# Relative-bias rows made in the first convolution layer and sent out from SBUF in sixteen pieces

## The chip, the cores and the metric

One Trainium2 chip, one core. The engines are TensorE (PE, with its weight loads PEld), VectorE (DVE), ScalarE (ACT) and GpSimd (POOL); SyncE (SP) issues nearly all DMA transfers, and 16 DMA engines move them. Each engine, and SP's queue, takes its instructions in order. The metric is the device time of one execution of the whole program in microseconds; the median of several runs counts.

## The reference

Two transformer blocks follow each other on 256 tokens of width 1024, batch 1, all in f32. The first block has two layers; each is a mixer and a convolutional feed-forward:

```
h = h + hgrn2_mixer(rms_norm(h))        # layer 0: a gated linear recurrence
h = h + conv_ffn(rms_norm(h))           # layer 0: (silu(conv(gate)) * conv(up)) @ w_down, conv of width 3
h = h + dsa_mixer(rms_norm(h))          # layer 1: attention on the 64 best keys of each query
h = h + conv_ffn(rms_norm(h))           # layer 1
```

The attention mixer scores all keys with 8 small index heads, keeps the top 64 keys of each query (`L // 4`), and does softmax attention with 16 heads over them. A bias that depends on the distance and the head is added to the logits:

```
rel = q_pos[None, :, None] - sel
bias = rel_bias.astype(jnp.float32)[t5_causal_bucket(rel)]     # rel_bias is (32 buckets, 16 heads)
logits = jnp.where(valid, logits + bias, NEG_BIG)
```

The second block (half-step SwiGLU layers, a gMLP mixer, a latent-attention mixer) is not touched.

## The kernel before

**Products.** Each f32 weight is split in two parts, `whi` and `wlo`, and each product is made of three matmuls (`whi` with both parts of x, `wlo` with one). A *unit* is one 1 MB tile of weights: `fetch` (line 207) issues its DMA on SP into one of three `wst` buffers, and `unit` (line 228) splits it: ACT copies `wst` to `whi` (line 249), DVE subtracts to get `wlo` (line 251). There are four `whi` and four `wlo` buffers. So the transfer of unit n is issued when DVE has split unit n-3, and ACT can split unit n when PE has finished unit n-4. A unit of a projection is 48 matmuls on PE (lines 263 to 265).

**The first convolution layer.** `conv_ffn` (line 663) loops over 11 pairs of gate and up units (22 units of `in_ffn_w_up`); after each unit DVE scales the sums (`cvx`, line 690) and DVE and ACT do the convolution (`cvg`, `cvu`, lines 671 to 673), the silu and the product, and split the result for the down projection (`in_ffn_w_down`, lines 565 to 567).

**The bias.** `rel_bias` (line 1044) is called after that layer. It loads a 0/1 table (`onehot`) and the 32 x 16 bias table (`rtab`), multiplies them on PE (line 1055) into 384 values for each head, copies them to SBUF (`rrow`, line 1057), and one DMA (line 1059) writes them to the DRAM tensor `bias_rows` of 16 heads x 128 query rows x 384: each head's row, which lies on one SBUF partition, is written 128 times over, 3 MB in all. The attention reads the bias back from there with a row step of 383 instead of 384, which shifts each query's row by one; these are 12 loads named `dx` (line 1166).

**The attention mixer.** `dsa` (line 1062) takes its units in this order: `dside` (keys and values), two units of index queries `dqi`, a half unit of values, and four units of queries (called q0 to q3 here; their results are `dq`, line 1152). The index scores are products on PE (line 1109), which ACT passes through a relu (`drl`, line 1112), and DVE sums over the index heads (`dsc`, lines 1116 and 1118) before it picks the 64 best (lines 1125 and 1126).

A scheduler sets the order of instructions on each engine when the program is built; `behind` (line 192) asks it not to place instructions ahead of PE's last one.

Of the kernel before, what the change touches and what calls it, by code (L numbers as in the profile page):

```python
# [7 lines left out]
F32 = mybir.dt.float32  # L8
# [7 lines left out]
P = 128  # L16
D = 1024
T = 256
KD = 8
# [3 lines left out]
NEG = -1e30  # L23
# [12 lines left out]

N_G, N_E, N_M, N_Z = 30, 4, 4, 2
N_SQ, N_WX, N_W, N_SM = 4, 3, 3, 3
ONCE = ("hrr", "hrh", "hrg", "dwt", "fgain", "f2", "mq1", "mq2", "mq3", "mq4", "mss", "dz")
N_TOP = 64  # L40
LEVELS = 5
CUTS = 4
# [76 lines left out]
C_ONEHOT = C_TRIL + P  # L119
# [28 lines left out]
class Net:  # L148
# [27 lines left out]
    def small(s, name, n):  # L176
        bufs = 1 if name in ONCE else N_SM
        return s.tp.tile([P, 16], F32, name=name, tag=name, bufs=bufs)[:, :n]
# [13 lines left out]
    def behind(s):  # L192

        pe = mybir.EngineType.PE
        return s.tc.issue_after(next(i for i in reversed(s.nc.cur_bb.bb.instructions) if i.engine == pe))

    def warm(s, n):

        if n:
            with s.behind():  # L200
                ps = s.prod()
                x = s.ident.bitcast(BF16)
                for _ in range(n):
                    s.nc.tensor.matmul(ps[:, :T], x[:, :P], x, start=True, stop=True)
# [180 lines left out]
    def pre(s, gain):  # L385
        p = Net.Pre()
        p.gain, p.ss, p.halves = gain, s.small("pss", 8), False
        p.marks, p.turns = [], []
        p.x = Split(s, "x", KD)
        return p  # L390
# [272 lines left out]
    def conv_ffn(s, p, l, out):  # L663
        nc, a = s.nc, s.a
        w = a["ffn_w_up"][l]
        hid = Split(s, "f", KF)
        s.begin(p)

        def conv(y, x, c):
            taps = [s.vec("conv_w%d%d" % (i, l), c, 1) for i in range(3)]  # L670
            nc.scalar.activation(y, x, AF.Identity, scale=taps[2], bias=s.vec("conv_b%d" % l, c, 1))
            nc.vector.scalar_tensor_tensor(y[:, 1:], x[:, :T - 1], taps[1], y[:, 1:], op0=OP.mult, op1=OP.add)
            nc.vector.scalar_tensor_tensor(y[:, 2:], x[:, :T - 2], taps[0], y[:, 2:], op0=OP.mult, op1=OP.add)

        h2 = lambda x: x.rearrange("p (j t) -> p j t", j=2)
        for i in range(KF // 2):
            if l == 0 and i in (3, 6):

                if i == 3:
                    turns = s.conv_vectors(1)  # L680
                else:
                    with s.behind():
                        for turn in turns:
                            turn()
            ys = [s.e("cvg"), s.m("cvu")]
            for y, first in zip(ys, (0, KF)):
                c = first + 2 * i
                ps = s.feat2(s.unit([(w, c * P, T)], 0, KD), p.x)
                x = s.z("cvx")
                nc.vector.tensor_tensor(h2(x), h2(ps), s.rb2(p), op=OP.mult)  # L690
                for j in range(2):
                    half = slice(j * T, (j + 1) * T)
                    conv(y[:, half], x[:, half], c + j)
                if not first:
                    nc.scalar.activation(y, y, AF.Silu)
            g, u = ys
            nc.vector.tensor_tensor(u, u, g, op=OP.mult)
            s.split(hid.hi.pair(i), hid.lo.pair(i), u)
        s.down(a["ffn_w_down"][l], hid, KF, out)
# [344 lines left out]
    def rel_bias(s):  # L1044


        nc, a = s.nc, s.a
        onehot = s.e("onehot")[:, :384]
        tab = s.tmp("rtab", P)
        nc.sync.dma_start(onehot, a["consts"][:, C_ONEHOT:])  # L1050
        nc.gpsimd.memset(tab, 0.0)
        nc.gpsimd.memset(tab[32:64], NEG)
        nc.sync.dma_start(tab[:32, :16], a["rel_bias"])
        ps = s.mix()
        nc.tensor.matmul(ps[:, :384], tab, onehot, start=True, stop=True)
        row = s.m("rrow")[:, :384]
        nc.vector.tensor_copy(row, ps[:, :384])
        scr = s.dp.tile([16, P, 384], F32, name="bias_rows")
        nc.sync.dma_start(scr, row[:16][:, None, :].to_broadcast([16, P, 384]))
        s.bias_rows = scr  # L1060

    def dsa(s, p, out_):
        nc, a = s.nc, s.a
# [606 lines left out]
def run_net(tc, a, out, stop=99, debug=None):  # L1670
    with ExitStack() as ctx:
        s = Net(tc, ctx, a)
        nc = tc.nc

        def dump(name):
            if debug and name in debug:
                nc.sync.dma_start(debug[name].rearrange("(t p) d -> p t d", p=P), s.h)
            return stop <= int(name[1:])

        w = a["hgrn_w_in"][0]  # L1680
        p = s.start([(w, D), (w, D + T), (w, D + 2 * T)])
        dump("h0")
        nxt = s.hgrn(p, s.first)
        if dump("h1"):
            return
        p = s.pre_end(nxt)
        nxt = s.pre(s.vec("attn_norm", KD))
        s.conv_ffn(p, 0, s.residual(nxt))
        s.rel_bias()
        if dump("h2"):  # L1690
            return
        p = s.pre_end(nxt)
        nxt = s.pre(s.vec("ffn_norm", KD))
        s.dsa(p, s.residual(nxt))
        if dump("h3"):
            return
        p = s.pre_end(nxt)
        out1, end1 = s.block1_end(s.vec("final_norm"), a["final_norm"], s.vec("pre_g", 0))
        s.conv_ffn(p, 1, out1)
        if dump("h4"):  # L1700
            return
        p = end1()
        dump("h5")
        wg, wu, wd = (a["ffn_w_%s_2" % n] for n in ("gate", "up", "down"))

        def ffn(p, l, j, pres, beside=None, **kw):
            s.swiglu(p, wg[l, j], wu[l, j], wd[l, j], s.post(a["ffn_post_g_2"][l, j], pres, True, **kw), beside)

        pre = lambda l, j: s.pre(s.vec("pre_g", (2 * l + j) * KD))
        mixg = lambda n, l: s.vec(n, l * KD)  # L1710
        nxt = s.pre(mixg("mix_pre", 0))
        kn = []
        ffn(p, 0, 0, [nxt])
        if dump("h6"):
            return
        p, nxt = nxt, pre(0, 1)
        s.gmlp(p, s.post(a["mix_post_g_2"][0], [nxt]))
        if dump("h7"):
            return
        p, nxt, kv = nxt, pre(1, 0), s.pre(s.vec("kv_norm"))  # L1720
        ffn(p, 0, 1, [nxt, kv])
        s.rope_tables()
        if dump("h8"):
            return
        ckv = []
        p, nxt = nxt, s.pre(mixg("mix_pre", 1))
        ffn(p, 1, 0, [nxt], lambda: ckv.extend(s.shared_kv(kv)), fill=lambda: kn.append(s.k_heads(ckv)))
        if dump("h9"):
            return
        p, nxt = nxt, pre(1, 1)  # L1730
        s.mla(p, ckv, kn[0], s.post(a["mix_post_g_2"][1], [nxt], late=L_MLA))
        if dump("h10"):
            return
        dst = out.rearrange("o (t p) d -> p (o t) d", p=P)

        def done(n, t):
            cols = slice(n * T, (n + 1) * T)
            nc.sync.dma_start(dst[:, t, cols], s.h[:, t, cols])


        ffn(nxt, 1, 1, [], done=done)
# [34 lines left out]
```

## Time and profile before

| | |
|---|---|
| median of 3 runs | 1652.7 us (1647.62 to 1656.69) |
| the profiled execution: time | 1660.22 us |
| the profiled execution: span, first to last instruction | 1658.4 us |
| PE busy in the span | 1622.1 us (98%) |
| DVE busy | 1150.2 us (69%) |
| ACT busy | 913.1 us (55%) |
| mean DMA rate | 179 GB/s |

The profiled execution stands 7.5 us above the median of the runs. Busy shares are means over the whole span, over stages with different limits. "Granted clock" is TensorE's clock as a share of its upper level (2.4 GHz); 0.50 is the lower level, 1.2 GHz.

### The profile page before, as it was taken

The numbers are of one execution on the slowest core, as the hardware profiler recorded it, in microseconds if no ns is written. First come the engines' busy times: TensorE is split into PE (matmuls) and PEld (weight loads), VectorE is DVE, ScalarE is ACT, GpSimd is POOL, SyncE is SP. The second block draws the span as 40 slices with busy tenths as digits, with TensorE's granted clock in tenths as the row PEclk, the third lists the DMA queues.
The fourth block names the chain that finished last, engine by engine and source line by source line (L and its number), as shares of the span: only waits on it lengthen the run. The fifth ranks groups of instructions, "written<-read, shape, count | busy, mean of one in ns | idle before, by whom it ended". The sixth has DMA issues, their size and how long they took to land.

```text
span 1658.4 us, 34159 instructions
## 1 busy us (share of the span) xinstructions
PE 1622.1 (98%) x14500; PEld 1608.4 (97%) x14502; DVE 1150.2 (69%) x1900; ACT 913.1 (55%) x1443; POOL 6.7 (0%) x28
## 2 busy tenths in 40 slices
PE   8989999996999999999999999999999999999998
PEld 8979999995999999999999999999999999999998
DVE  6997899545769975766668757664676647576643
ACT  7876665443666555544466446444664448574442
POOL 0000000000000000000000000000000000000000
PEclk9999999997999999999999999999999999999999
DMA  8733655677546556556756556556475665446551
GB/s 266 220 97 114 200 178 188 191 141 177 157 149 208 173 181 216 182 186 217 231 161 211 168 175 197 186 169 206 130 233 189 193 201 151 132 153 212 189 190 58
DMA packets 303821, 297.58 MB, mean 179 GB/s; under 512 B 14295, under 2 KB 300214, under 8 KB 303670
## 3 DMA queue, kind: packets, MB, share of 16 engines
q1 hardware_dynamic: 303622, 295.40, 57.4%
q8 instruction: 114, 1.87, 0.5%
q14 instruction: 37, 0.30, 0.1%
q10 hardware_dynamic: 48, 0.01, 0.0%
HBM read 291.19 MB, written 4.19 MB: 178 GB/s over the span
## 4 chain that ended last, share of the span: by engine, by line
PE 88%; DVE 4%; DMA 3%; ACT 3%; issue 1%; SPq 0%; DVEq 0%; ACTq 0%
PE acc L263 16%; PE acc L265 16%; PE acc L264 16%; PE acc L565 8%; PE acc L567 7%; PE acc L566 7%; PE acc L289 2%; PE acc L290 2%; PE acc L291 2%; DMA bias_rows<-rrow 2%; PE acc L576 2%; PE acc L578 2%; PE acc L577 2%; DVE wlo L251 1%; ACT whi L249 1%
## 5 line engine op out<-in xcount | busy, mean ns | idle before, releaser
L249 ACT ACTIVATE whi<-wst 128x2048 fp32r<-128x2048 f32 (+4 forms) x404 | 523.8, 1330 | 517.5 <-issue 228.6
L251 DVE TENSOR_TENSOR wlo<-wst,whi 128x2048 fp32r<-128x2048 f32 (+4 forms) x404 | 621.0, 1561 | 251.6 <-ACT whi L249 249.6
L264 PE MATMUL acc<-xl,whi 128*128 128x256 f32 x2416 | 675.2, 280 | 1.1 <-DVE xl L308 1.1
L263 PE MATMUL acc<-xh,whi 128*128 128x256 f32 x2416 | 675.3, 281 | 0.8 <-ACT xh L306 0.4
L265 PE MATMUL acc<-xh,wlo 128*128 128x256 f32 x2416 | 674.7, 280 | 0.5 <-DVE wlo L251 0.5
L264 PEld LDWEIGHTS acc<-xl,whi 128*128 128x128 f32 x2416 | 458.1, 190 | 1.7 <-DVE xl L308 1.5
L265 PEld LDWEIGHTS acc<-xh,wlo 128*128 128x128 f32 x2416 | 455.0, 189 | 0.9 <-DVE wlo L251 0.7
L263 PEld LDWEIGHTS acc<-xh,whi 128*128 128x128 f32 x2416 | 454.3, 188 | 1.6 <-ACT xh L306 0.7
L567 PE MATMUL acc<-wlo,fh 128*128 128x256 f32 x880 | 245.3, 279 | 0.0
L565 PE MATMUL acc<-whi,fh 128*128 128x256 f32 x880 | 244.7, 279 | 0.0
L566 PE MATMUL acc<-whi,fl 128*128 128x256 f32 x880 | 244.5, 278 | 0.0
L567 PEld LDWEIGHTS acc<-wlo,fh 128*128 128x128 f32 x880 | 165.2, 188 | 0.0
L565 PEld LDWEIGHTS acc<-whi,fh 128*128 128x128 f32 x880 | 165.0, 188 | 0.0
L566 PEld LDWEIGHTS acc<-whi,fl 128*128 128x128 f32 x880 | 164.9, 187 | 0.0
L289 PE MATMUL acc<-whi,xh 128*128 128x256 f32 x384 | 108.9, 284 | 0.0
L291 PE MATMUL acc<-wlo,xh 128*128 128x256 f32 x384 | 106.8, 278 | 0.0
L290 PE MATMUL acc<-whi,xl 128*128 128x256 f32 x384 | 106.8, 278 | 0.0
L289 PEld LDWEIGHTS acc<-whi,xh 128*128 128x128 f32 x384 | 72.1, 188 | 0.2
L290 PEld LDWEIGHTS acc<-whi,xl 128*128 128x128 f32 x384 | 72.1, 188 | 0.0
L291 PEld LDWEIGHTS acc<-wlo,xh 128*128 128x128 f32 x384 | 72.1, 188 | 0.0
L658 DVE TENSOR_TENSOR ffu<-acc,rb 128x512 f32<-128x512 f32 x41 | 28.3, 691 | 48.5 <-PE acc L265 48.3
L308 DVE SCALAR_TENSOR_TENSOR xl<-mx,vectors,xh 128x128 fp32r<-128x128 f32 (+1 forms) x124 | 39.1, 376 | 23.1 <-ACT xh L306 23.0
(422 smaller groups left out, 2097.3 us busy)
## 6 DMA issues: line engine op xcount, KB each, us to landing
wst<-in_ffn_w_up_dram SPq DMA_DIRECT2D x88, 1024.0 KB, 5.2
wst<-in_ffn_w_down_dram SPq DMA_DIRECT2D x48, 1024.0 KB, 5.9
wst<-in_ffn_w_gate_dram SPq DMA_DIRECT2D x44, 1024.0 KB, 5.4
wst<-in_ffn_w_down_dram SPq DMA_DIRECT2D x24, 768.0 KB, 4.8
wst<-in_gmlp_w_in_dram SPq DMA_DIRECT2D x16, 1024.0 KB, 5.4
wst<-in_hgrn_w_in_dram SPq DMA_DIRECT2D x13, 1024.0 KB, 5.5
wst<-in_gmlp_w_out_dram SPq DMA_DIRECT2D x8, 1024.0 KB
wst<-in_dsa_w_in_dram SPq DMA_DIRECT2D x6, 1024.0 KB
```

Of the source, the lines that this page charges most:

```text
L249: s.nc.scalar.activation(hi[:, c], w[:, c], AF.Copy)
L251: s.nc.vector.tensor_tensor(lo[:, c], w[:, c], hi[:, c].bitcast(F32), op=OP.subtract)
L263: mm(ps, wh[:, k, cols], xh, start=k == 0, stop=False)
L264: mm(ps, wh[:, k, cols], xl, start=False, stop=False)
L265: mm(ps, wl[:, k, cols], xh, start=False, stop=k == nk - 1)
L289: mm(ps, xh[:, ts], wk, start=k == 0, stop=False)
L290: mm(ps, xl[:, ts], wk, start=False, stop=False)
L291: mm(ps, xh[:, ts], lk, start=False, stop=k == nk - 1)
L308: b = s.nc.vector.scalar_tensor_tensor(lo, src, g, hi.bitcast(F32), op0=OP.mult, op1=OP.subtract)
L565: mm(ps[t], xh, wh[:, k], start=k0 + k == 0 and not both, stop=False)
L566: mm(ps[t], xl, wh[:, k], start=False, stop=False)
L567: mm(ps[t], xh, wl[:, k], start=False, stop=k0 + k == kn - 1 and (t == 1 or not both))
```

## The change

`rel_bias` now makes no instruction by itself: it returns a list of 18 steps, which `conv_ffn` of layer 0 takes one by one. The first loads the two tables (in the pair of units i = 1, behind the fetch of its gate unit), the second is the product on PE and the copy to `rrow` (i = 1, up unit), and the other sixteen each write 8 query rows of all 16 heads to `bias_rows`, 192 KB, one behind the fetch of each unit from i = 3 to i = 10. `after_fetch` asks the scheduler not to place a step ahead of SP's last DMA. `rrow` has a buffer of its own, of which only 16 partitions are copied; the room comes from three small tiles (`ss2`, `gmv`, `grs`) that now have one buffer instead of three. The bytes that are written are the same.

```diff
-ONCE = ("hrr", "hrh", "hrg", "dwt", "fgain", "f2", "mq1", "mq2", "mq3", "mq4", "mss", "dz")
+ONCE = ("hrr", "hrh", "hrg", "dwt", "fgain", "f2", "mq1", "mq2", "mq3", "mq4", "mss", "dz", "ss2", "gmv", "grs")
...
+    def after_fetch(s):
+
+        sp = mybir.EngineType.SP
+        return s.tc.issue_after(next(i for i in reversed(s.nc.cur_bb.bb.instructions) if i.engine == sp))
...
+        bias = s.rel_bias() if l == 0 else []
...
-                ps = s.feat2(s.unit([(w, c * P, T)], 0, KD), p.x)
+                u = s.unit([(w, c * P, T)], 0, KD)
+                if bias and (i > 2 or i and len(bias) > 16):
+                    with s.after_fetch():
+                        bias.pop(0)()
+                ps = s.feat2(u, p.x)
...
-        ps = s.mix()
-        nc.tensor.matmul(ps[:, :384], tab, onehot, start=True, stop=True)
-        row = s.m("rrow")[:, :384]
-        nc.vector.tensor_copy(row, ps[:, :384])
+        row = s.tp.tile([P, 384], F32, name="rrow", tag="rrow", bufs=1)
         scr = s.dp.tile([16, P, 384], F32, name="bias_rows")
-        nc.sync.dma_start(scr, row[:16][:, None, :].to_broadcast([16, P, 384]))
         s.bias_rows = scr
...
+        def product():
+            onehot, tab = parts
+            with s.behind():
+                ps = s.mix()
+                nc.tensor.matmul(ps[:, :384], tab, onehot, start=True, stop=True)
+            nc.vector.tensor_copy(row[:16], ps[:16, :384])
+
+        def spread(q):
+            nc.sync.dma_start(scr[:, q:q + 8], row[:16][:, None, :].to_broadcast([16, 8, 384]))
+
+        return [load, product] + [lambda q=q: spread(q) for q in range(0, P, 8)]
...
         s.conv_ffn(p, 0, s.residual(nxt))
-        s.rel_bias()
```

SP's queue around the attention mixer before: the write of `bias_rows` stands ahead of the weights of q2 (the row behind it), the four `dx` loads of the first block of queries and the weights of q3.

```order
L216 DMA wst<-in_dsa_w_in_dram 128x8x128
L216 DMA wst<-in_dsa_w_in_dram 128x8x256 x2
L1059 DMA bias_rows<-rrow 2048x1x384
L216 DMA wst<-in_dsa_w_in_dram 128x8x256
L1166 DMA dx<-bias_rows 128x4x128 x4
L216 DMA wst<-in_dsa_w_in_dram 128x8x256
L216 DMA wst<-in_dsa_w_out_dram 128x8x256 x3
```

The same place in the changed program:

```order
L221 DMA wst<-in_dsa_w_in_dram 128x8x128
L221 DMA wst<-in_dsa_w_in_dram 128x8x256 x3
L1187 DMA dx<-bias_rows 128x4x128 x4
L221 DMA wst<-in_dsa_w_in_dram 128x8x256
L221 DMA wst<-in_dsa_w_out_dram 128x8x256 x3
```

The write has left the place; q0, q1 and q2 follow each other, and the rest keeps its order.

SP's queue in the up projection of the first convolution layer, changed program, from the first of the 22 units on; before, the 22 `wst` loads stand here with `rtab` behind the third and nothing else between them:

```order
L221 DMA wst<-in_ffn_w_up_dram 128x8x256 x3
L1068 DMA rtab<-in_rel_bias_dram 32x16
L465 DMA vst<-in_ffn_conv_w_dram 44x128
L465 DMA vst<-in_ffn_conv_b_dram 44x128
L221 DMA wst<-in_ffn_w_up_dram 128x8x256 x4
L1065 DMA onehot<-in_consts_dram 128x384
L221 DMA wst<-in_ffn_w_up_dram 128x8x256 x2
L1079 DMA bias_rows<-rrow 16x8x384 x3
L221 DMA wst<-in_ffn_w_up_dram 128x8x256
L1079 DMA bias_rows<-rrow 16x8x384
```

Three pieces stand behind the ninth unit's load, and from there each of the 13 other loads has one piece behind it. The two `vst` loads (convolution taps of layer 1) stood further ahead before.

DVE in the changed program, in the same stretch; the row on `rrow` is new here, and before it stood at the start of the attention mixer:

```order
L678 SCALAR_TENSOR_TENSOR cvu<-cvx,vectors,cvu 128x255 x2
L1076 COPY rrow<-mx 16x384
L256 TENSOR_TENSOR wlo<-wst,whi 128x2048
L700 TENSOR_TENSOR cvx<-acc,rb 128x512
L679 SCALAR_TENSOR_TENSOR cvu<-cvx,vectors,cvu 128x254 x2
```

One copy of 16 partitions is put between a convolution step and the split of the seventh unit. Further on in this layer the scheduler also places two `cvx` rows behind each other in most pairs, where they stood apart before.

## Rows read from the trace of the kernel before

**Rows 1.** The page: the chain that ended last, shares by engine and line.
```profile
PE 88%; DVE 4%; DMA 3%; ACT 3%; issue 1%; SPq 0%; DVEq 0%; ACTq 0%
PE acc L263 16%; PE acc L265 16%; PE acc L264 16%; PE acc L565 8%; PE acc L567 7%; PE acc L566 7%; PE acc L289 2%; PE acc L290 2%; PE acc L291 2%; DMA bias_rows<-rrow 2%; PE acc L576 2%; PE acc L578 2%; PE acc L577 2%; DVE wlo L251 1%; ACT whi L249 1%
```

**Rows 2.** The chain from 340 to 400 us: start, duration, what.
```profile
350.84 32.55 DMA bias_rows<-rrow
...
385.54 7.77 DMA wst<-in_dsa_w_in_dram
```

**Rows 3.** SP's timeline from 340 to 400 us: start, duration, line, transfer.
```profile
351.61 9.49 SPq L216 DMA_DIRECT2D wst<-in_dsa_w_in_dram  x1
383.41 2.02 SPq L1166 DMA_DIRECT2D dx<-bias_rows  x4
385.54 1.04 SPq L216 DMA_DIRECT2D wst<-in_dsa_w_in_dram  x1
```

**Rows 4.** ACT's timeline, same stretch; in brackets the idle time before and its releaser.
```profile
366.11 0.18 ACT L1088 ACTIVATE dwt<-mx 128x16 f32<-128x16 f32 x1
386.81 1.91 ACT L249 ACTIVATE whi<-wst 128x2048 fp32r<-128x2048 f32 x1 [20.51 <-DMA wst<-in_dsa_w_in_dram]
```

**Rows 5.** PE's timeline, same stretch.
```profile
368.17 1.05 PE L1109 MATMUL pr<-dki,dqi 128*128 128x128 f32 x8
...
372.60 0.28 PE L263 MATMUL acc<-xh,whi 128*128 128x256 f32 x1
389.04 2.07 PE L1109 MATMUL pr<-dki,dqi 128*128 128x128 f32 x8 [16.17 <-ACT drl L1112]
390.77 0.56 PE L264 MATMUL acc<-xl,whi 128*128 128x256 f32 x1
...
394.12 0.28 PE L264 MATMUL acc<-xl,whi 128*128 128x256 f32 x1
...
395.65 1.99 PE L1109 MATMUL pr<-dki,dqi 128*128 128x256 f32 x8 [0.30 <-ACT drl L1112]
```

**Rows 6.** Stretches: length, busy time of each engine, granted clock, DMA share, GB/s.
```profile
376.00:380.00 4.00, 0.00 (x0) 0.00 (x0) 0.00 (x0) 0.00 (x0) 0.00 (x0) 0.63 0.90 103
...
390.00:392.00 2.00, 2.00 (x12) 2.00 (x11) 1.86 (x4) 0.00 (x0) 0.00 (x0) 0.50 1.09 348
```

**Rows 7.** DVE's timeline from 355 to 450 us.
```profile
361.57 2.29 DVE L251 TENSOR_TENSOR wlo<-wst,whi 128x2048 fp32r<-128x2048 f32 x1 [1.07 <-ACT whi L249]
...
368.37 0.69 DVE L1098 TENSOR_TENSOR dqi<-acc,rb 128x512 f32<-128x512 f32 x1 [1.15 <-PE acc L265]
388.75 2.29 DVE L251 TENSOR_TENSOR wlo<-wst,whi 128x2048 fp32r<-128x2048 f32 x1 [19.69 <-ACT whi L249]
...
395.36 2.29 DVE L251 TENSOR_TENSOR wlo<-wst,whi 128x2048 fp32r<-128x2048 f32 x1 [2.88 <-ACT whi L249]
...
413.77 0.67 DVE L1152 SCALAR_TENSOR_TENSOR dq<-acc,rb 128x512 f32<-128x512 f32 x1
```

**Rows 8.** A stretch of the first convolution layer's up projection, columns as in rows 6.
```profile
180.00:270.00 90.00, 90.00 (x767) 90.00 (x766) 85.37 (x120) 58.76 (x68) 0.00 (x0) 1.00 0.62 198
```

**Rows 9.** DMA from 185 to 260 us: rate in 40 slices; issues with KB, us to landing.
```profile
GB/s 288 346 238 370 143 198 360 2 187 367 10 200 353 15 173 368 19 169 374 16 157 376 34 170 371 18 153 378 37 102 382 76 0 164 373 123 375 92 72 327
...
wst<-in_ffn_w_up_dram SPq DMA_DIRECT2D x13, 1024.0 KB, 5.1
```

**Rows 10.** The up projection: SP's issue of one unit, ACT's and DVE's split of it.
```profile
193.74 6.02 SPq L216 DMA_DIRECT2D wst<-in_ffn_w_up_dram  x2
206.43 1.92 ACT L249 ACTIVATE whi<-wst 128x2048 fp32r<-128x2048 f32 x1 [0.29 <-PE acc L264]
208.38 2.29 DVE L251 TENSOR_TENSOR wlo<-wst,whi 128x2048 fp32r<-128x2048 f32 x1 [0.19 <-ACT whi L249]
```

**Rows 11.** DMA issues of the whole span: KB each, us from issue to landing.
```profile
out_dram<-h SPq DMA_DIRECT2D x8, 128.0 KB, 1.8
```

**Rows 12.** The product for the bias on PE, two matmuls: ns min/median/max, starts.
```profile
L1055 PE MATMUL mx<-onehot,rtab x2: 486/487/488, 349.3 to 349.6; 128*128 128x384 f32 x2
```

More of the change, by code (lines that the diff above doesn't have):

```diff
@@ L1047, in rel_bias, with load @@
         nc, a = s.nc, s.a
[L1048 to L1053, printed above, removed]
-        ps = s.mix()
-        nc.tensor.matmul(ps[:, :384], tab, onehot, start=True, stop=True)
-        row = s.m("rrow")[:, :384]
-        nc.vector.tensor_copy(row, ps[:, :384])
+        row = s.tp.tile([P, 384], F32, name="rrow", tag="rrow", bufs=1)
         scr = s.dp.tile([16, P, 384], F32, name="bias_rows")
-        nc.sync.dma_start(scr, row[:16][:, None, :].to_broadcast([16, P, 384]))
         s.bias_rows = scr
+        parts = []
+        def load():
+            onehot, tab = s.e("onehot")[:, :384], s.tmp("rtab", P)
+            nc.sync.dma_start(onehot, a["consts"][:, C_ONEHOT:])
+            nc.gpsimd.memset(tab, 0.0)
+            nc.gpsimd.memset(tab[32:64], NEG)
+            nc.sync.dma_start(tab[:32, :16], a["rel_bias"])
+            parts.extend((onehot, tab))
+        def product():
[7 more added lines that the diff above has]
+        return [load, product] + [lambda q=q: spread(q) for q in range(0, P, 8)]
     def dsa(s, p, out_):
```

## The prediction

> **What bounds the kernel now.** I read the chain that ended last first: 88% of the span is PE's, spread evenly over the products, and the one transfer with a share of its own is `bias_rows`, 2% [rows 1]. 2% of 1658 us is 33 us, so I went to where it stands in time. In the chain of that stretch the write begins at 350.84 and takes 32.55 us, and the next link but the `dx` issues is a load of `in_dsa_w_in` [rows 2]. SP's timeline tells what the write does to its neighbours [rows 3]: the weights of q2 are issued right behind it, at 351.61, and that one issue takes 9.49 us; the `dx` loads wait until the write has landed, 383.41; the weights of q3 stand behind them, 385.54. ACT's timeline shows the harm: the split of q2 starts at 386.81 after 20.51 us in which ACT waited for that transfer [rows 4]. The relu `drl` is behind the split in ACT's order, PE's second batch of index scores waits for `drl`, and PE stands still for 16.17 us, up to 389.04 [rows 5]. The stretches show PE without a single matmul from 376 to 380 us, and a granted clock that falls and is 0.50, the lower level of 1.2 GHz, also after PE has begun again [rows 6]. So in a kernel whose PE is 98% busy this is one real hole, and what ends it last is a transfer and not an engine.
>
> **What the change removes.** The write, from SP's place ahead of q2. Three terms of PE's time hang on it.
> (a) The idle time: 16.17 us [rows 5].
> (b) The lower clock behind it. From 389.04 to 394.12 PE does one batch of 8 small products and 15 matmuls in 5.08 us [rows 5]. The same batch took 1.05 us at 368.17 [rows 5], and 15 matmuls at the pace of the up projection, 90 us for 767 or 0.117 us each [rows 8], take 1.76 us. 5.08 - 1.05 - 1.76 = 2.3 us.
> (c) The wait of the third batch for ACT, which waited for the weights of q3: 0.30 us [rows 5].
> Sum 18.8 us.
>
> **What is late next.** Without the write the weights of q2, issued at 351.6, land some 5.1 us later like other 1 MB loads [rows 9], at 357. ACT needs a free `whi` buffer too: q2 is the mixer's seventh unit, so that is when PE has finished the third, whose sums DVE takes at 368.37 [rows 7]. The split then runs from 368.4 to 370.3, `drl` follows, and PE, which comes to its second batch at 372.7 (372.60 plus one step), finds it done. So (a) goes whole.
> The weights of q3 stay behind the four `dx` loads. Those need the buffer of `dside`, which ACT has read by 366.3 [rows 4]; the `wst` buffer of q0 is free at 361.57 + 2.29 = 363.9 [rows 7]. Issue then at 366.5 at the latest. Landing: at best 5.1 us later, 371.6; at worst what `dx`, q2 and q3 together took, from 383.41 to 385.54 + 7.77 = 393.3 [rows 2, 3], which is 9.9 us, so 376.4. ACT's split takes 1.9 us and `drl` about 0.5: ready between 374.0 and 378.8. PE comes to the third batch 395.65 - 389.04 - 2.3 - 0.3 = 4.0 us behind the second [rows 5], at 376.7. PE thus waits 0 to 2.1 us; since q2's part of those 9.9 us is now moved beforehand, I take 0.3.
> DVE has a chain of its own there, the search of the 64 best. From the split of q2 at 388.75 to the end of the `dq` at 413.77 + 0.67 it takes 25.7 us, 2.9 of them idle, so 22.8 of work [rows 7]. It can start at 370.3 and end at 393.1. PE needs for the same stretch 25.4 us less (b) and (c), 22.8, and comes there at 395.5: 2.4 us of room, so DVE stays behind PE's pace by little. Gain 18.8 - 0.3 = 18.5 us.
>
> **What it adds.** The product: two matmuls of 0.49 us [rows 12], taken from the mixer and put in the up projection, where PE is as busy (90 of 90 us, [rows 8]); sum 0. The copy to `rrow` is DVE's, half a microsecond where DVE has 4.6 us free in 90 [rows 8]. Table loads and memsets are moved, not added; PE's uses of the tables are far behind.
> The pieces are what could cost. One is a sixteenth of the write: 32.55 / 16 = 2.03 us of the DMA engines [rows 2]. In the up projection a unit is 48 matmuls, 5.63 us of PE. Its load moves 1 MB at about 376 GB/s (the full slices show 367 to 382, [rows 9]): 2.8 us, and the slices between them are nearly empty. 2.8 + 2.03 = 4.83 of 5.63 us: the loads and pieces fit behind each other. Bounds: at least 192 KB at the loads' rate, 0.5 us; at most the 2.03 us plus the whole issue-to-landing time of a small store, 1.8 us [rows 11], as if the ring stood still meanwhile: 3.83. I take 2.03, since pieces read the same 16 partitions as the write did.
> The cover, if they take more: a load issued at 193.74 lands at 198.8, and ACT starts on it at 206.43, when PE frees the buffer, not the transfer [rows 9, 10]; 7.6 us. DVE is done at 208.38 + 2.29 = 210.7 [rows 10], and PE comes to that unit three units after 206.43, at 223.3; 12.6 us more. PE starves only when the pieces have put the loads back by 20.2 us: 16 x (2.8 + x - 5.63) > 20.2, x > 4.1 us per piece. Even the upper bound stays below. So 0.
> Three pieces leave together behind the ninth load, once the copy is made: 6 us at once, inside the 7.6. The tenth load is queued behind their wait on SP, and ACT is the one that would wait for it; it has the same cover.
> DVE's new order (two `cvx` behind each other) lets DVE stand until PE ends the next unit, up to the free 4.6 us in 90; its splits are finished 12.6 us before PE needs them, so PE sees nothing of it: 0, at worst 2 us.
>
> **Weighed against the Trainium skill.** The page "SBUF — State Buffer", section "The DMA setup-cost knee", speaks against the change: every transfer pays about 2 us that do not shrink with its size, so few large ones are to be preferred. By that rule sixteen pieces cost some 30 us more than one write; an estimate from that page is 2.03 + 2 = 4.03 us per piece, and by it the sum would still be 18.5 us, 16 x 1.2 = 19.2 us of delay being under 20.2, but with nothing to spare. The trace shows fixed time too, a load of 2.8 us landing after 5.1 [rows 9], but whether it holds the engines no row of before says.
>
> **The rivals.**
> 1. *The pieces crowd the weights, slower than before.* Place: the load ring in the up projection; deciding point x: PE starves from 4.1 us per piece on, and the gain is eaten at 16 x (x - 2.83) - 20.2 = 18.5, x = 5.2 us. For it: the write ran at a quarter of the loads' rate (3 MB in 32.55 us). Against it: nothing in the rows reaches 5.2. At x = 6 the loss is 50.7 - 20.2 = 30.5 us, the time 1652.7 - 18.5 + 30.5 = 1665; at x = 4.6 it is 8 us and 1642.
> 2. *Another link is late in the mixer.* q3's weights (2.1 us), DVE's chain (2.4 us of room, so 2 to 3 us if it starts late) and the new order (2 us) could each keep some: gain 12 to 16, time 1637 to 1641. For it: DVE and PE are within 2.4 us of each other. Against it: DVE starts further ahead of PE than it did.
> 3. *The hole stays.* q2's load would be as late for another reason, say a long issue by itself. Against it: 9.49 us of issue is seen only behind the write, whose transfer the ring was still moving. Time 1652.
>
> **How the numbers follow.** The sum is made on the profiled execution: 1660.2 - 18.5 = 1641.7 us of time. That execution lies 7.5 us above the median of the runs, and a hole is the same in both, so the median goes from 1652.7 to 1634.2. Chances: the forecast 0.76, rival 2 0.12, rival 1 0.08 (half of it slower than before), rival 3 0.04. The likeliest case alone reaches from 1630 to 1639, half from the runs' own spread of 9 us. The range takes in rival 2 and the light half of rival 1: 1629 to 1645. What a measurement can tell from no change is about 0.5%, 8.3 us, so faster means below 1644.4: forecast, rival 2 and a little of rival 1, 0.88; within it 0.07; slower 0.05.
>
> **What would show it.** Right: no transfer of `bias_rows` after some 275 us; ACT's split of q2 starting at about 368 behind PE, not behind a DMA; the granted clock at 1.00 through the mixer; PE at 90 of 90 us in the up projection, ACT's splits there still released by PE; pieces near 2 us. Wrong: splits in the up projection released by `wst` transfers and PE idle there (rival 1), or PE waiting in the mixer for `drl`, `dq` or `pen` (rival 2).

## The result, and the profile after

The changed kernel takes 1630.8 us in the median of four runs (1630.66 to 1632.06), the kernel before 1652.2 us beside it (1647.62 to 1656.69): ratio 0.986, 95% interval 0.9833 to 0.9887. The prediction was 1634.2 us, with a range of 1629 to 1645. The profiled execution took 1630.7 us, with a span of 1628.9 us.

The page: busy time of the engines, and the shares of the chain that ended last.

```profile
PE 1608.4 (99%) x14500; PEld 1595.2 (98%) x14502; DVE 1150.0 (71%) x1900; ACT 913.4 (56%) x1443; POOL 6.8 (0%) x28
...
PE 95%; DVE 2%; ACT 1%; issue 1%; DMA 0%; SPq 0%; DVEq 0%; ACTq 0%
```

The 2% of `bias_rows` and the 3% of DMA in [rows 1] are gone. In the mixer the places to look at are those of [rows 3 to 6]. First SP's timeline (start, duration, line, transfer), then ACT's splits of q2 and q3 with the relus behind them, then PE's three batches of index scores (no bracket means no idle time), then two of the stretches of [rows 6].

```profile
343.57 10.04 SPq L221 DMA_DIRECT2D wst<-in_dsa_w_in_dram  x3
353.66 12.90 SPq L1187 DMA_DIRECT2D dx<-bias_rows  x4
366.66 0.45 SPq L221 DMA_DIRECT2D wst<-in_dsa_w_in_dram  x1
```

```profile
370.23 1.92 ACT L254 ACTIVATE whi<-wst 128x2048 fp32r<-128x2048 f32 x1 [1.77 <-issue]
372.05 0.64 ACT L1133 ACTIVATE drl<-pr 128x256 f32<-128x256 f32 x2
373.95 1.92 ACT L254 ACTIVATE whi<-wst 128x2048 fp32r<-128x2048 f32 x1 [1.26 <-issue]
375.76 0.64 ACT L1133 ACTIVATE drl<-pr 128x256 f32<-128x256 f32 x2
```

```profile
370.10 1.05 PE L1130 MATMUL pr<-dki,dqi 128*128 128x128 f32 x8
374.64 1.06 PE L1130 MATMUL pr<-dki,dqi 128*128 128x128 f32 x8
378.36 1.89 PE L1130 MATMUL pr<-dki,dqi 128*128 128x256 f32 x8
```

```profile
376.00:380.00 4.00, 4.00 (x31) 3.82 (x29) 3.50 (x5) 0.93 (x3) 0.00 (x0) 1.00 0.84 281
390.00:392.00 2.00, 2.00 (x19) 2.00 (x19) 1.97 (x9) 1.75 (x4) 0.00 (x0) 1.00 0.04 8
```

From the first batch to the third PE took 395.65 - 368.17 = 27.48 us before [rows 5] and takes 378.36 - 370.10 = 8.26 us now. That is 19.2 us less, where the terms (a), (b) and (c) add up to 18.8. ACT's bracket at q2 was 20.51 us behind a DMA [rows 4]; now it is 1.77 us, and not behind a transfer.

In the up projection: the stretch of [rows 8], the transfers from 185 to 260 us as in [rows 9] (KB each, us from issue to landing), and three of ACT's splits there.

```profile
180.00:270.00 90.00, 90.00 (x764) 89.73 (x763) 83.76 (x118) 57.56 (x66) 0.00 (x0) 1.00 0.74 231
```

```profile
wst<-in_ffn_w_up_dram SPq DMA_DIRECT2D x13, 1024.0 KB, 6.8
bias_rows<-rrow SPq DMA_DIRECT2D x16, 192.0 KB, 5.9
```

```profile
199.36 1.92 ACT L254 ACTIVATE whi<-wst 128x2048 fp32r<-128x2048 f32 x1 [4.04 <-DMA wst<-in_ffn_w_up_dram]
204.29 1.92 ACT L254 ACTIVATE whi<-wst 128x2048 fp32r<-128x2048 f32 x1 [1.51 <-DMA wst<-in_ffn_w_up_dram]
...
214.51 1.92 ACT L254 ACTIVATE whi<-wst 128x2048 fp32r<-128x2048 f32 x1 [2.07 <-PE acc L269]
```

PE is busy for 90 of 90 us, as before. But two splits now wait for their weights, those of the tenth and the eleventh unit, right behind the three pieces that leave together: the pieces used up ACT's part of the cover at once, and PE's part of it held. By the third split shown, PE releases ACT again.

### The profile page after: what moved, and what is told of

It reads as the page before. It is cut to its first block, busy times and chain, and to the rows that moved or that the text cites. A ratio compares the mean times of both kernels' runs of the same rounds, so it can differ in the third digit from the quotient of the medians.

```text
span 1628.9 us, 34166 instructions
## 1 busy us (share of the span) xinstructions
PE 1608.4 (99%) x14500; PEld 1595.2 (98%) x14502; DVE 1150.0 (71%) x1900; ACT 913.4 (56%) x1443; POOL 6.8 (0%) x28
## 4 chain that ended last, share of the span: by engine, by line
PE 95%; DVE 2%; ACT 1%; issue 1%; DMA 0%; SPq 0%; DVEq 0%; ACTq 0%
PE acc L268 17%; PE acc L270 17%; PE acc L269 17%; PE acc L570 8%; PE acc L571 8%; PE acc L572 8%; PE acc L294 3%; PE acc L296 3%; PE acc L295 3%; PE acc L583 2%; PE acc L581 2%; PE acc L582 2%; PE mx L417 1%; PE acc L1195 1%; PE mx L1223 1%
## 5 line engine op out<-in xcount | busy, mean ns | idle before, releaser
L663 DVE TENSOR_TENSOR ffu<-acc,rb 128x512 f32<-128x512 f32 x41 | 28.3, 691 | 44.6 <-PE acc L270 44.5
L313 DVE SCALAR_TENSOR_TENSOR xl<-mx,vectors,xh 128x128 fp32r<-128x128 f32 (+1 forms) x124 | 39.1, 375 | 21.5 <-ACT xh L311 21.4
```

The lines of the kernel that those rows point to most:

```text
L313: b = s.nc.vector.scalar_tensor_tensor(lo, src, g, hi.bitcast(F32), op0=OP.mult, op1=OP.subtract)
```

## The experiments

Medians of the runs, each with the ratio to runs of the kernel before that were taken beside it. Lines of code that only serve to fit an edit in are left out of the diffs; "..." stands for lines left out.

| kernel | median, us | ratio, 95% interval |
|---|---|---|
| sixteen pieces at the old place | 1657.95 | 1.0014, 0.9997 to 1.003 |
| one write in the up projection | 1648.19 | 0.9962, 0.9941 to 0.9984 |
| pieces fourfold | 1685.32 | 1.0172, 1.015 to 1.0193 |
| write behind q3 | 1657.01 | 1.0009, 0.9989 to 1.0029 |
| write on a queue of its own | 1647.58 | 0.9968, 0.9949 to 0.9987 |
| write from 128 partitions, old place | 1634.03 | 0.9888, 0.9865 to 0.991 |
| changed kernel again | 1628.78 | 0.9845, 0.9823 to 0.9867 |
| pieces twice | 1634.24 | 0.988, 0.9855 to 0.9905 |
| changed kernel, third time | 1630.24 | 0.9861, 0.9835 to 0.9887 |
| one write from 128 partitions, up projection | 1632.10 | 0.9882, 0.9856 to 0.9907 |
| pieces thrice | 1653.49 | 1.0001, 0.9988 to 1.0015 |

**Sixteen pieces at the old place.** Only the cut, without the move:

```diff
-        nc.sync.dma_start(scr, row[:16][:, None, :].to_broadcast([16, P, 384]))
+        for q in range(0, P, 8):
+            nc.sync.dma_start(scr[:, q:q + 8], row[:16][:, None, :].to_broadcast([16, 8, 384]))
```

> The kernel before, with its one write of 3 MB cut into the same sixteen pieces of 192 KB, one behind the other at the old place. Theory A (the place counts: the weights of q2 are queued behind 3 MB): the pieces take as long as the write, 16 x 2.03 = 32.5 us, q2's split on ACT starts at about 387, PE stands still for some 16 us, 1652 us. Rival B (pieces are cheaper in themselves: in the changed kernel's up projection they added only 74.0 - 61.2 = 12.8% of 90 us, 11.5 us, to the DMA engines' packet time): the pieces drain in 11 to 16 us, q2 lands by 370 to 373, PE's hole is 0 to 4 us, 1633 to 1640 us.

The hole is there in full. SP's timeline, ACT's split of q2, and what PE waited for in the mixer (us in total, times, longest):

```profile
347.13 27.13 SPq L1060 DMA_DIRECT2D bias_rows<-rrow  x16
374.36 1.83 SPq L216 DMA_DIRECT2D wst<-in_dsa_w_in_dram  x1
```

```profile
383.63 1.91 ACT L249 ACTIVATE whi<-wst 128x2048 fp32r<-128x2048 f32 x1 [21.04 <-DMA wst<-in_dsa_w_in_dram]
```

```profile
PE pr L1110 <- ACT drl L1113: 17.0, 2, 16.7
```

So the cut gains nothing by itself. One behind the other, a piece's issue takes 1.88 us (the median of the sixteen), as long as 192 KB take at 104 GB/s: SP gets on no faster than the pieces move. That is a piece's price alone, where the prediction took 2.03. Rival B fell here.

**One write in the up projection.** Only the move, without the cut:

```diff
-            nc.sync.dma_start(scr[:, q:q + 8], row[:16][:, None, :].to_broadcast([16, 8, 384]))
+            nc.sync.dma_start(scr[:, q:q + P], row[:16][:, None, :].to_broadcast([16, P, 384]))
...
-        return [load, product] + [lambda q=q: spread(q) for q in range(0, P, 8)]
+        return [load, product, lambda: spread(0)]
```

> The changed kernel, with one write of 3 MB behind the ninth load of the up projection in place of sixteen pieces behind thirteen loads. Theory A (the ring stands for the write's 32.6 us): the tenth load, which would land some 5 us after its issue at 188, lands at 186 + 32.6 + 2.8 = 221, 28 us late; cover 7.6 + 12.6 = 20.2 us; PE stands still for some 8 us there and 1 or 2 us more go to the lower clock: 1639 to 1641 us. Rival B (beside loads a write costs a third of that): the load is 12 to 16 us late, inside the cover, PE does not stand, 1631 us.

ACT's split of the tenth unit, what PE waited for, and the stretch of the hole:

```profile
221.86 1.91 ACT L254 ACTIVATE whi<-wst 128x2048 fp32r<-128x2048 f32 x1 [24.07 <-DMA wst<-in_ffn_w_up_dram]
```

```profile
PE acc L268 <- ACT whi L254: 12.0, 1, 12.0
PE acc L270 <- DVE wlo L256: 1.5, 1, 1.5
```

```profile
211.00:231.00 20.00, 6.50 (x37) 6.01 (x36) 7.20 (x9) 8.52 (x9) 0.00 (x0) 0.66 0.88 239
```

The load landed at about 221.8 us, when its split starts, where 221 was worked out. PE stands for 13.5 us, not 8. Issued at 185.99, the load would land at 191.1 by the 5.1 us of [rows 9]; it is 30.7 us late and costs 13.5, so the cover (the delay of a load that PE does not feel) at this place is 17.2 us and not 20.2. The 37 matmuls of the stretch took 6.50 us, 4.3 at the pace of [rows 8]: 2.2 us more for the lower clock. 15.7 us in all, of the 17 to 19 between the medians. The move without the cut thus keeps a quarter of the gain.

**Pieces fourfold, twice and thrice.** The bytes of each piece once, twice and three times more, to tensors that nothing reads (`range(3)` for fourfold):

```diff
-        parts = []
+        parts, more = [], [s.dp.tile([16, P, 384], F32, name="more%d" % i) for i in range(3)]
...
             nc.sync.dma_start(scr[:, q:q + 8], row[:16][:, None, :].to_broadcast([16, 8, 384]))
+            for other in more:
+                nc.sync.dma_start(other[:, q:q + 8], row[:16][:, None, :].to_broadcast([16, 8, 384]))
```

> The changed kernel, with every piece written four times (three more times to DRAM tensors that nothing reads): 768 KB behind each load. Theory A (2.03 us of the DMA engines per piece, deciding point 4.1 us): 8.1 us per unit, PE starves for 16 x (2.8 + 8.1 - 5.63) - 20.2 = 64 us, 1695 us. Rival B (0.7 us per piece, as the packet time of the changed kernel shows): 2.9 + 2.8 = 5.7 us per unit of 5.63, PE does not starve or by under 2 us, 1631 to 1633 us. In between, 1640 to 1680: pieces of 1 to 1.8 us.

> The changed kernel with each piece written twice (once more to a DRAM tensor that nothing reads). By the fourfold run a unit with four pieces and a load took 8.6 us of SP's queue, (8.6 - 2.8) / 4 = 1.45 us per piece: 2.8 + 2 x 1.45 = 5.7 us for 5.63, 1 us late in sixteen, and six pieces at once behind the ninth load, 9 to 11 us, inside a cover of 16 to 20: loss 0 to 2 us. By the 2.03 us of the prediction, 4.06 per unit, the loads come 16 x 1.23 = 19.7 us late: loss 0 to 4 us, at its edge. A loss of 10 us or more would say that a piece costs more than either.

> The changed kernel with each piece written three times (two more times to DRAM tensors that nothing reads). With 1.45 us per piece (fourfold run) a unit takes 2.8 + 3 x 1.45 = 7.15 us for 5.63, sixteen of them come 24.3 us late, the cover is 16 to 20: PE waits 4 to 8 us, and some 2 to 4 us more go to the lower clock: 1634 to 1642 us. With 2.03 us per piece: 8.9 us, 52 us late, PE waits 32 to 36 us, 1661 to 1670 us. No wait at all would say that pieces cost under 1.1 us.

SP's issue of the first piece behind a load in the first and in the thirteenth of those units, and the stretch with the stalls, fourfold:

```profile
208.17 1.98 SPq L1079 DMA_DIRECT2D bias_rows<-rrow  x1
...
311.85 1.47 SPq L1079 DMA_DIRECT2D bias_rows<-rrow  x1
```

```profile
210.00:320.00 110.00, 81.70 (x588) 79.23 (x587) 61.24 (x86) 41.05 (x49) 0.00 (x0) 0.88 0.89 216
```

The same, thrice:

```profile
202.28 2.05 SPq L1079 DMA_DIRECT2D bias_rows<-rrow  x1
...
280.83 2.10 SPq L1079 DMA_DIRECT2D bias_rows<-rrow  x1
```

```profile
200.00:320.00 120.00, 105.97 (x870) 104.16 (x868) 90.19 (x129) 63.66 (x75) 0.00 (x0) 0.97 0.84 237
```

Twelve units take 103.7 us fourfold, 8.64 each; less the 2.8 us of the load that is 1.46 us per piece. Thrice they take 78.55 us, 6.55 each, 1.25 us per piece. Beside loads a piece is cheaper than alone, and all of it below 2.03. In the changed kernel itself, with one piece to a unit, the DMA share rose from 0.62 [rows 8] to 0.74 of the 90 us, which is 0.7 us for each of the sixteen. With two pieces to a unit PE waits for nothing in the up projection; with three it stands 14.0 us of these 120, with four 28.3 of 110. Fourfold, another 12.7 us go to the lower clock (588 matmuls are 69.0 us at the pace of [rows 8]).

The forecast for fourfold, 1695, was near, and for a wrong reason: with 1.46 us per piece the same sum gives 16 x (8.64 - 5.63) - 20.2 = 28 us, and the burst behind the ninth load, twelve pieces that go out from 185 to 206 us before the tenth load, and the lower clock come on top; 55 us were measured. Thrice was a miss: 23 us above the changed kernel measured beside it, where 4 to 12 were expected. ACT's split of the tenth unit in that run, two of DVE's steps behind it, PE's first wait, and PE's largest sum of waits from 170 to 450 us:

```profile
210.52 1.92 ACT L254 ACTIVATE whi<-wst 128x2048 fp32r<-128x2048 f32 x1 [15.66 <-DMA wst<-in_ffn_w_up_dram]
212.47 2.29 DVE L256 TENSOR_TENSOR wlo<-wst,whi 128x2048 fp32r<-128x2048 f32 x1 [13.62 <-ACT whi L254]
...
215.68 0.69 DVE L700 TENSOR_TENSOR cvx<-acc,rb 128x512 f32<-128x512 f32 x1
```

```profile
216.51 0.36 PE L268 MATMUL acc<-xh,whi 128*128 128x256 f32 x1 [3.24 <-DVE cvx L700]
```

```profile
PE acc L268 <- DVE cvx L700: 11.4, 7, 3.2
```

The burst is nine pieces here. Without it the tenth load, issued some 2.2 us behind the first piece at 185.21 as in the changed kernel and landing 5.1 us later, would land at some 192.5 (an estimate from these rows); it is 18 us late, which alone is more than the cover of 17.2. Each of the next twelve units then adds 6.55 - 5.63 = 0.92 us, together 11. That makes about 12 of the 14.0 us. Of the other 9 us between the medians some 4 go to the lower clock (870 matmuls are 102.1 us at the pace of [rows 8]); the rest was not accounted for. The rows also show a link that the sums leave out: PE mostly does not wait for the weights that are late but for `cvx`, which stands behind the split of the late unit in DVE's order. Fourfold it is the same, 20.9 us of PE's 33.7 from 170 to 450 us.

The deciding point lies between two pieces per unit (2.5 to 2.9 us at these prices) and three (3.75), a little below the 4.1 us of the forecast. Two per unit came out 5.5 us above the changed kernel measured beside it, with runs that overlap and no wait of PE; 0 to 2 were expected, and what the 5.5 are was not shown.

By the Trainium skill ("SBUF — State Buffer", section "The DMA setup-cost knee") each transfer pays about 2 us of fixed time, most of it completion latency; the prediction's estimate from that page put them on the DMA engines. The 1.88 us of a piece alone and the 1.25 to 1.46 beside loads leave no room for that: in these runs, between transfers that are queued back to back, it is hidden.

**Write behind q3.** The kernel before, with the four loads of q0 to q3 fetched first:

```diff
-        nc.sync.dma_start(scr, row[:16][:, None, :].to_broadcast([16, P, 384]))
...
+        fetched = [s.fetch([(w, i * T, T)], 0, KD) for i in range(4)]
+        with s.after_fetch():
+            nc.sync.dma_start(scr, s.row[:16][:, None, :].to_broadcast([16, P, 384]))
```

> The kernel before, with the write of 3 MB in one piece and in the same mixer, but issued behind the weights of q2 and q3; the dx loads follow it. Theory A (what hurts is what stands behind the write in the queue): q2 and q3 are on time, terms (a), (b) and (c) of 18.8 us come back; the write is issued at some 364 to 367, lands at 397 to 400, the dx loads at some 402 to 404, and the first use of dx, at 396 in the changed kernel, is 6 to 8 us late and holds PE: 1638 to 1642 us. Rival C (the bandwidth that the write takes hurts, wherever it stands in the mixer): w_out's loads and dx are crowded, PE loses 15 us or more again, 1648 to 1655 us.

ACT's timeline, and what PE waited for:

```profile
374.51 0.60 ACT L1117 ACTIVATE drl<-pr 128x512 f32<-128x512 f32 x1 [0.27 <-PE pr L1114]
400.06 2.19 ACT L254 ACTIVATE whi<-wst 128x512 fp32r<-128x512 f32 x4 [24.95 <-DMA wst<-in_dsa_w_out_dram]
402.16 1.06 ACT L1117 ACTIVATE drl<-pr 128x512 f32<-128x512 f32 x2
```

```profile
PE acc L1178 <- DVE pen L1135: 18.6, 1, 18.6
```

The time is that of rival C, and the mechanism is that of A with a link that I had missed. q2 and q3 were on time, and PE waited only once from 340 to 430 us. The next weights, `in_dsa_w_out`, came to stand behind the write; ACT's order has their split ahead of the last two relus, DVE's search waited for the relus, and PE for `pen`. The hole moved one load on and kept its size.

**Write on a queue of its own.** The kernel before; SP's queue then holds only weights there (the access pattern of `dx` is left out, `bass.AP(...)`):

```diff
-        nc.sync.dma_start(scr, row[:16][:, None, :].to_broadcast([16, P, 384]))
+        nc.scalar.dma_start(scr, row[:16][:, None, :].to_broadcast([16, P, 384]))
...
-            nc.sync.dma_start(x, bass.AP(...))
+            (nc.gpsimd if at < 4 else nc.sync).dma_start(x, bass.AP(...))
```

> The kernel before, with the one write of 3 MB at its old time but issued on ACT's queue, and the four dx loads that need it on GpSimd's queue; the orders of ACT's, DVE's and PE's work stay as before, and SP's queue holds only weights there. Theory A (the harm is to what stands behind the write in its queue): q2, q3 and w_out go past the write. They share the DMA engines with it and land later than 5 us after their issue, but q2's weights, issued at 351, have until 368: PE stands still for 0 to 3 us, 1631 to 1638 us. Rival C (the harm is the share of the DMA engines that the write takes, on whatever queue): q2 lands when the write is nearly through, at 380 or later, PE stands still for 10 us or more, 1644 to 1655 us.

SP's issue of q3's load, the DMA queues from 362 to 374 us (packets, MB, share of 16 engines), ACT's split of q3, and PE's third batch:

```profile
361.66 0.37 SPq L216 DMA_DIRECT2D wst<-in_dsa_w_in_dram  x1
```

```profile
DMA packets 788, 1.23 MB, mean 102 GB/s; under 512 B 0, under 2 KB 787, under 8 KB 787
...
q10 hardware_dynamic: 787, 1.21, 89.7%
```

```profile
384.85 1.91 ACT L249 ACTIVATE whi<-wst 128x2048 fp32r<-128x2048 f32 x1 [16.32 <-DMA wst<-in_dsa_w_in_dram]
```

```profile
387.08 3.33 PE L1109 MATMUL pr<-dki,dqi 128*128 128x256 f32 x7 [12.71 <-ACT drl L1112]
```

Neither theory was right alone. The load of q2, issued 0.3 us behind the write, ran beside it (from 350 to 361 us q1, SP's queue, has 31.6% of the packet time, and q10, the write, 68.4%), and q2's batch came without a wait. q3's load was issued at 361.66 on a queue with nothing ahead of it, and from 362 to 374 us not one packet of q1 is in the trace; q10 has all but one of the 788. By the 5.1 us of [rows 9] it would have landed at 366.8; its split starts at 384.85, 18 us late, and PE waits 12.7 us, so the cover here is some 5 us. So SP's order is not the whole cause: the write holds the DMA engines, at 102 GB/s and a share of 0.9, and a load on another queue can wait all the same. The Trainium skill ("DMA: Bandwidth & Descriptors", section "Issuing engines are not separate DMA queues") has transfers of all issuing engines run on the same 16 DMA engines, and the row agrees. The same page's section "Queues, rings and completion order" has each DMA engine take turns between the queues that have work; for q2's load that fits, for the 12 us of q3's this run does not show it.

**Write from 128 partitions, old place.** The kernel before; the table is tiled, so that every partition holds a head's row:

```diff
+        few = s.small("rfew", 16)
+        nc.sync.dma_start(few[:32], a["rel_bias"])
+        nc.gpsimd.tensor_copy(tab[:32].rearrange("p (h r) -> p h r", r=8), few[:32, :, None].to_broadcast([32, 16, 8]))
...
-        nc.sync.dma_start(scr, row[:16][:, None, :].to_broadcast([16, P, 384]))
+        nc.sync.dma_start(scr.rearrange("h (r q) c -> (h r) q c", r=8), row[:, None, :].to_broadcast([P, 16, 384]))
```

> The kernel before, with the write at its old place in one piece, but sent from all 128 partitions: the table is tiled eight times, so that partition 8h + r holds head h's row and is written 16 times over. Theory D (the 104 GB/s of the write are those of 16 partitions): 3 MB at some 330 to 376 GB/s, as the loads reach, take 8 to 10 us, q2 lands by 366 and the dx loads by 370, no hole: 1631 to 1636 us. Rival E (the rate is that of packets of 1536 bytes, or of writes to DRAM): 30 us or more again, 1652 us.

SP's timeline, ACT's splits of q2 and q3, and a stretch of the write:

```profile
347.05 0.62 SPq L1061 DMA_DIRECT2D bias_rows<-rrow  x1
347.76 3.01 SPq L216 DMA_DIRECT2D wst<-in_dsa_w_in_dram  x1
359.34 2.02 SPq L1168 DMA_DIRECT2D dx<-bias_rows  x4
```

```profile
364.51 1.91 ACT L249 ACTIVATE whi<-wst 128x2048 fp32r<-128x2048 f32 x1 [2.00 <-issue]
369.35 1.92 ACT L249 ACTIVATE whi<-wst 128x2048 fp32r<-128x2048 f32 x1 [2.38 <-DMA wst<-in_dsa_w_in_dram]
```

```profile
348.00:356.00 8.00, 8.00 (x72) 8.00 (x71) 1.35 (x5) 1.38 (x4) 0.00 (x0) 1.00 0.99 351
```

Same place, same bytes, one transfer: the `dx` loads, which wait for the write, start 12.3 us behind its issue, 32.6 before [rows 2, 3], and PE waits for nothing in the mixer. Packets of some 1.5 KB to the same DRAM tensor move at 351 GB/s here (1828 packets, 2.81 MB in the 8 us) and at 104 in the kernel before (936 packets, 1.44 MB from 366 to 380 us), so rival E falls: the slow rate was that of 16 partitions. The Trainium skill ("SBUF — State Buffer", section "Door 1: The DMA port swizzle") gives 104 GB/s for 16 partitions from 0 on and 328 for all 128, at 1 MiB; 102 and some 351 GB/s here agree. The gain, 1653.19 - 1634.03 = 19.2 us, is what the mixer had to give. The changed kernel's second set of runs, taken beside this one, lies 5.2 us lower still; no wait of PE tells the two apart (PE is idle for 20.6 us of the profiled span here and 20.8 there).

**One write from 128 partitions, in the up projection.** Both edits together:

> The changed kernel with one write of 3 MB from 128 partitions behind the ninth load of the up projection, in place of sixteen pieces from 16 partitions. Theory F (what counts is only how long the DMA engines are held against the cover of that place): the write holds them 8.6 us as at the old place, the tenth load lands some 6 to 9 us late, inside a cover of 16 to 20 us; PE does not wait, 1625 to 1632 us, as the changed kernel. Rival G (16 pieces between the loads are needed, a write in one piece costs at this place whatever its rate): PE waits 5 us or more there, 1635 us or more.

PE waits for nothing from 170 to 450 us; ACT waits once for a load, 2.4 us. 1632.1 us beside 1630.2 of the changed kernel, runs from 1630 to 1642 and 1624 to 1637: not to be told apart. One transfer at more than three times the rate does what sixteen pieces do. No version tried beats the changed kernel.

**The changed kernel again, twice.** Nothing edited:

> The changed kernel once more, unaltered, for its own spread and for TensorE's pace at a granted clock of 1.00, which was 5.44 us per unit in some stretches and 5.65 us in others of the same execution. If the pace is a matter of the execution and not of the change: the runs spread by 5 us or more, as those of the kernel before do (1647 to 1661), around 1631 to 1637 us. If the change settles the pace: all runs within 2 us of 1631 us, as its first four were.

> The changed kernel unaltered, beside the two below on the same chip, and for TensorE's pace. From its nine runs so far: 1624 to 1632 us, no wait of PE from 180 to 430 us, and the stretches of the faster and the slower pace in other places than in its first two profiles, with the mixer at the same length of 155 to 156 us.

The fifteen runs lie between 1624.2 and 1636.5 us; 66 runs of the kernel before between 1645.6 and 1661.5. The runs are not all within 2 us, as the first four were: the pace is not the change's (below). Nor did they all fall where expected: the second set lies from 1624.8 to 1629.6, below the 1631 to 1637, and the third reaches 1636.5, above 1632. PE waits for nothing from 170 to 430 us in either. From the first batch to the third PE took 371.92 - 363.87 = 8.05 us in the profile of the third time.

## Why the prediction was right

**What bounds the kernel.** Right: the hole was the write's, and with it gone the chain has no transfer in it.

**Terms (a), (b), (c).** 18.8 us were worked out less 0.3 for a wait of q3. Measured on PE's batches: 19.2, and no wait for q3. The spot values hold too: q2's split was set at 368.4 and stands at 370.23, in a program that is 1.9 us later at that place (first batch at 370.10, at 368.17 before [rows 5]).

**The whole gain.** 18.5 us forecast; the three pairs of medians differ by 21.4, 24.4 and 22.0. The mixer accounts for 19.2. The other 2 to 5 us are no wait: over the whole span PE is idle for 1658.4 - 1622.1 = 36.3 us before and for 20.5, 20.8 and 20.6 us in the three profiles of the changed kernel, and the difference of 15.5 to 15.8 is no more than the hole. The rest lies in the busy time of the same 14500 matmuls, and the kernels' paces (last section) differ by as much from execution to execution. That the medians differ by it, too, was not shown. It was by the same token luck that the forecast, made on an execution 7.5 us above the median, came out so near: the profiled executions differ by 29.5 us, 15.8 of them idle time, 2.3 the lower clock (b) and 11.4 the rest of the busy time.

**The pieces.** The term was over-sized: 2.03 us taken, 1.88 measured alone and 1.25 to 1.46 beside loads; it changed nothing, as the sum was 0 either way. The cover was over-sized too, 20.2 us taken and 17.2 measured. And the sum of the deciding point counts 16 units with one piece each, where 13 loads follow three pieces: the last of them is 15 x - 12 x 2.83 us late, which is 20.2 at x = 3.6 us and not 4.1. So the upper bound of 3.83 did not stay below it, as the prediction says; the 2.03 taken do, with room. The tell-tale "ACT's splits there still released by PE" was wrong: the prediction said that the 7.6 us of ACT's cover would hold the three pieces that leave together, and ACT waited 4.04 and 1.51 us. If pieces grow, the burst uses the cover first (thrice, above), and the steady rate comes on top.

**The cause, one step deeper.** The prediction put the harm down to the order in SP's queue. The runs say: 3 MB from 16 partitions hold the DMA engines for 32 us, and a load issued after it, on SP's queue (pieces at the old place, write behind q3) or on another (q3's load, though not q2's), costs PE what its delay exceeds its cover by: 17.2 us of cover in the up projection, some 5 for q3. The change moves the write between loads that have the 17.2 us and cuts it so that no load has more than a burst of three pieces ahead of it; the move alone kept a quarter of the gain, the cut alone none, and the full rate alone gave all that the mixer had to give.

**Rivals.** Rival 1 is real, though not at the size of this change: larger pieces make PE wait at its place and nearly at its deciding point, and with two per unit PE still waits for nothing. Rivals 2 and 3 did not come up.

## What to carry to other kernels

Price a long transfer by how long it holds the DMA engines, and put that against the cover of the loads issued after it; a queue of its own freed one of them here and not the next. Moving it one load back only moves the hole to the next load that an in-order engine meets. Look at its rate first: a write at 102 GB/s from 16 partitions ran at 351 from 128, and then PE waited for it neither at the old place nor at the new one. When it is cut into pieces, the burst at the start uses the cover before the steady rate does.

## What was not expected of the hardware

At a granted clock of 1.00 and PE busy throughout, TensorE runs the same matmuls at two paces. SP's issues of the units in one late feed-forward, which PE paces, in the kernel before and in the changed one:

```profile
1032.79 0.37 SPq L216 DMA_DIRECT2D wst<-in_ffn_w_gate_dram  x1
1038.44 0.37 SPq L216 DMA_DIRECT2D wst<-in_ffn_w_up_dram  x1
```

```profile
1015.24 0.37 SPq L221 DMA_DIRECT2D wst<-in_ffn_w_gate_dram  x1
1020.68 0.37 SPq L221 DMA_DIRECT2D wst<-in_ffn_w_up_dram  x1
```

5.65 us per unit in the one, 5.44 in the other: 3.7% less. It is not the program alone: the changed kernel, run a third time, has this in the stretch where it had 764 matmuls the first time.

```profile
180.00:270.00 90.00, 90.00 (x792) 89.73 (x791) 85.66 (x119) 60.13 (x71) 0.00 (x0) 1.00 0.77 241
```

Each profiled execution has stretches of some hundred microseconds at either pace. They are not always in other places, as was expected: the first two profiles of the changed kernel agree in six stretches from 180 to 1600 us to within one matmul, and the third differs from them by 28 matmuls in this one and by at most 9 in the others. PE's busy time differs by 6.6 us between the first and the third profile and their times by 6.5. The runs of one kernel differ by 12 to 16 us; that the pace makes all of that was not shown. What switches it stays open; the granted clock does not show it. So stages are compared here, and not whole spans.

Open too is why q3's load moved no packet for 12 us beside the write on another queue, when q2's did.
